# Transposed dense products as three passes of 256 columns into one sum, activation tiles at one place modulo 512 bytes

## The chip, the cores and the metric

The kernel runs on one core of one Trainium2 chip. The metric is the device time of one execution in microseconds (us), as the median of repeated runs.

## The reference

A two-layer trunk for 256 tokens of 2048 features, in float32:

```
for i in range(DEPTH):                      # DEPTH = 2
    h = rms_norm(x, mixer_norm[i])
    x = x + (diff_attention(h, ...) if i % 2 == 0 else gated_deltanet(h, ...))
    x = x + conv_ffn(rms_norm(x, ffn_norm[i]), ...)

def conv_ffn(h, w_up, conv_w, conv_b, w_down):
    u = causal_dwconv(h @ w_up, conv_w) + conv_b
    val, gate = jnp.split(u, 2, axis=-1)
    return (jax.nn.silu(gate) * val) @ w_down
```

Both mixers begin and end with dense products too: queries, keys, values and the output of the attention; queries, keys, values, gates, z and the output of the delta rule. Nearly all of the arithmetic is in these dense products with float32 weights.

## The kernel before, in words

Activations lie transposed, with the features on the 128 partitions and the 256 tokens along the free axis. A weight matrix comes in blocks of 256 output features and, within a block, in chunks of 512 KB (four tiles of 128 input features, `CK = 4`). `weights` (L67) issues the load of a chunk on SyncE's queue into `raw`, ScalarE casts it to the rounded part `whi` (L78), and VectorE subtracts to get the rest, `wlo` (L79). `raw` has four buffers, `whi` and `wlo` three each. An activation is split in the same way, and its two parts lie side by side in one tile of 512 columns: `h` (16 tiles h0 to h15, the input of a stage), `ac` (the attention's outputs, and the products of the gated MLP), `oc` (outputs of the delta rule). A product of two such numbers is the sum of three terms: hi times hi, lo (weight) times hi, hi times lo (activation).

`dense` (L92) forms a block. It has a PSUM bank of 512 columns for each of the two tiles of 128 features, numbered c, and for each tile k of the input and each c it does one *step*:

- in the form with two halves, two matmuls: `whi` against both parts at once, 512 columns wide (L112), and `wlo` against the first part, 256 columns wide, into the second half of the bank (L115). The two halves are added afterwards, in `merge` (L123) by ScalarE and VectorE, or in `add_out` (L232) by two additions.
- in the folded form (`fold=True`), three matmuls of 256 columns, all into the first half of the bank (L107, L108, L109), so that nothing is left to add.

Each matmul has its own load of 128 columns of weights into the array (PEld in the profile). The folded form is used in the gated delta rule, for the products with `w_in` (tiles `h`) and `w_out` (tiles `oc`), and for the very last block of the second MLP. All else that is transposed has two halves: `w_qk` (16 blocks of 32 steps), `w_o` (8 blocks of 32 steps), `w_up` of both MLPs (43 blocks of 32 steps each), `w_down` of both (8 blocks of 86 steps, the last block of the second MLP folded) and the gates of the delta rule (16 steps). That is 512 + 256 + 2752 + 1290 + 16 = 4826 steps with two halves and 1024 + 512 + 86 folded ones. `dense_tok` (L129), for values and z, is of another kind: there the weights move, 512 columns wide, and the activations are loaded into the array.

The stages follow each other: attention, MLP 0, delta rule, MLP 1. Matmuls between the dense ones (scores, norms, the small inverses of the delta rule) run as generators in the background, a step after each chunk (`tick`). In an MLP the only background work is `norm_stat` (L170): the sum over the partitions of the squares, with one matmul of 256 columns (L182) and two of one column (L184), after the third chunk of the stage. A scheduler orders the instructions of each engine.

Of the kernel before, what the change touches and what calls it, by code (L numbers as in the profile page):

```python
# [8 lines left out]
F32 = mybir.dt.float32  # L9
# [7 lines left out]
P = 128  # L17
# [8 lines left out]
class Trunk:  # L26
    """Activations lie transposed, features on the partitions and the 256 tokens along the free axis.

    A float32 operand of a dense product is split into two float32r parts (hi + lo, exact), and
    the passes carry hi * hi, hi * lo and lo * hi; the parts of an activation lie side by side, so  # L30
    that one pass of a weight's hi takes both, and the two halves of the sum are added after. Work that follows a dense block and needs the
    tensor engine again runs as a generator in the background, a step after each chunk of weights.
    """
# [33 lines left out]
    def weights(self, ap):  # L67
        """A chunk [128, k, n] of weights, in two parts."""
        nc = self.nc
        nk, n = ap.shape[1:]  # L70

        def tile_(tag, dt, bufs):
            t = self.wp.tile([P, CK * T], dt, tag=tag, name=tag, bufs=bufs)
            return t[:, :nk * n].rearrange("p (k n) -> p k n", n=n)

        raw, hi, lo = tile_("raw", F32, 4), tile_("whi", F32R, 3), tile_("wlo", F32R, 3)
        nc.sync.dma_start(raw, ap)
        nc.scalar.copy(hi, raw)  # L78
        nc.vector.tensor_tensor(lo, raw, hi.bitcast(F32), ALU.subtract)  # L79
# [10 lines left out]
    def dense(self, w, kt, acts, tiles=2, fold=False, lead=0):  # L90
        """out^T of 128 * tiles features, a PSUM bank for each 128, in two halves to be added,
        or (fold) in one, which spares the vector engine the sum."""  # L92
        nc = self.nc
        ps = self.banks()
        for k0, nk in self.chunks(kt, CK, lead):
            hi, lo = self.weights(w[:, k0:k0 + nk, :])
            steps = [(k, c) for k in range(nk) for c in range(tiles)]
            if fold and k0 + nk == kt:
                steps = [(k, c) for c in range(tiles) for k in range(nk)]
            for k, c in steps:  # L100
# [3 lines left out]

                def sole():
                    o = ps[:, c, :T]
                    nc.tensor.matmul(o, hi[:, k, s], a[:, 0, :], start=first, stop=False)  # L107
                    nc.tensor.matmul(o, lo[:, k, s], a[:, 0, :], start=False, stop=False)  # L108
                    nc.tensor.matmul(o, hi[:, k, s], a[:, 1, :], start=False, stop=last)  # L109

                def one():
                    nc.tensor.matmul(ps[:, c, :], hi[:, k, s], a, start=first, stop=last)  # L112

                def two():
                    nc.tensor.matmul(ps[:, c, T:], lo[:, k, s], a[:, 0, :], start=False, stop=False)  # L115

                for f in ((sole,) if fold else (one, two) if first else (two, one)):
                    f()
# [3 lines left out]
    def merge(self, ps, u):  # L122
        """The two halves of a dense block, added and divided by the rms of the tokens."""  # L123
        nc = self.nc
# [24 lines left out]
    def norm_tile(self, k, gcol):  # L149
        """One tile of x * gain, split; 1 / rms is applied after the products."""  # L150
# [19 lines left out]
    def norm_stat(self, wait=1):  # L170
        """1 / rms of each token, over all partitions and as columns."""
# [22 lines left out]
    def lnexp(self, inst):  # L194
        """After inst, the activations within run from the table set that has both functions."""
# [4 lines left out]
    def conv(self, out, u, taps, bias):  # L200
        """Causal depthwise convolution along the tokens."""
# [10 lines left out]
    def rsqrt(self, out, ps, n):  # L212
        """(ps / n + eps) ** -0.5"""
# [4 lines left out]
    def split(self, out, a):  # L218
        """Two float32r parts of a, out[:, 0] + out[:, 1] = a."""
# [3 lines left out]
    def total(self, out, parts):  # L223
        """Sums over the partitions of tiles, in two parts each, on every partition."""
# [6 lines left out]
    def add_out(self, blk, ps, done, fold=False):  # L231
        """x += a block of a projection, and what follows on each finished tile of x."""  # L232
        x = self.x[:, 2 * blk:2 * blk + 2, :]
        for i in range(1 if fold else 2):
            self.nc.vector.tensor_tensor(x, ps[:, :, i * T:(i + 1) * T], x, ALU.add)  # L235
# [5 lines left out]
    def project(self, w, kt, acts, done, final=False):  # L241
        """x += a projection; with final, the last block is left a tile at a time."""
# [3 lines left out]
        if final:  # L246
            ps = self.dense(w[n - 1], kt, acts, fold=True)
# [31 lines left out]
    def attention(self, w_qk, w_v, w_o, nh, dist_ap, ident_ap, qg, kg, lvec, sub, start, done, lambda_init):  # L279
        """qg, kg, lvec (4 columns), sub (2 columns): per-partition columns."""  # L280
        nc, mp = self.nc, self.mp
        with self.tc.tile_pool(name="at", bufs=1) as at:
# [5 lines left out]
            dist = at.tile([P, 384], F32, tag="dist", name="dist")  # L288
# [44 lines left out]
            def weigh(h, qn, kn, go, aT):  # L333
                """The differential attention weights of a head, keys on the partitions."""
# [77 lines left out]
    def gdn(self, w_gate, w_in, w_z, w_out, nb, hb, gate_ap, const_ap, hot_ap, conv_col, ng, done):  # L412
        """nb batches of hb query/key heads, each with two value heads; 128 wide, all of them.

        const_ap: identity, mask of the decays, upper triangle of ones.
        All 256 tokens are one chunk: u = (I + strict(K K^T . D) beta)^-1 v, o = (Q K^T . D) beta u, with
        D_ij = exp(G_i - G_j) for i >= j, beta within the exponent. Matrices lie transposed, as
        [second half of the keys: 128 queries | first half: 256 queries].
        """
# [5 lines left out]
        with tc.tile_pool(name="gd", bufs=1) as gd:  # L425
            self.spawn(self.norm_stat())
            con = gd.tile([P, 384], F32, tag="con", name="con")
# [18 lines left out]
            def lin(ps):  # L446
                u = gd.tile([P, 2, T], F32, tag="u", name="u", bufs=2)
                nc.vector.tensor_tensor(u, ps[:, :, :T], self.rstd.unsqueeze(1).to_broadcast([P, 2, T]), ALU.mult)
# [9 lines left out]
            def keys(hq, c, cc, b0, res):  # L458
                """Decayed K K^T and Q K^T of the two value heads of a query/key head."""
# [52 lines left out]
            def invert(cc, lqs, inv):  # L512
                """Inverses of the unit lower triangular 32x32 blocks on the diagonal, one in a partition."""
# [23 lines left out]
            def levels(TT, Ta, lts, ttc, tcc, m0):  # L537
                """Transposes of the inverses of the 128x128 blocks, from those of the 32x32 ones."""
# [54 lines left out]
            def group(gi, gr, lqs, inv, vt, ready, zts, acts):  # L593
                """Outputs of the value heads of a group, on their way to the last projection."""
# [67 lines left out]
            def out(b, acts):  # L662
                for blk in range(KD // 2):
                    ps = self.dense(w_out[b * (KD // 2) + blk], 2 * hb, lambda k: self.await_(acts, k), fold=True)
                    self.add_out(blk, ps, done if b == nb - 1 else None, True)
# [4 lines left out]
            for b in range(nb):  # L670
# [6 lines left out]
                for op, i in plan + [("v", i) for i in range(1, hb)]:  # L677
                    if op == "k":
                        hq = heads[i]
                        c = convs(lin(self.dense(w_in[hq * 2], KD, self.h_acts, fold=True)), (hq, nq + hq))  # L680
# [10 lines left out]
                    else:  # L691
# [7 lines left out]
                        c = convs(lin(self.dense(w_in[hq * 2 + 1], KD, self.h_acts, fold=True)),  # L699
# [7 lines left out]
    def gates(self, gd, pg, nv, gp, ident, triu, res):  # L707
        """Cumulated log decays as rows (two parts on 64 partitions), and negated, with the log of beta, as columns."""
# [200 lines left out]
```

## Time and profile before

| | |
|---|---|
| median of 3 runs | 2741.3 us (2741.16 to 2741.84) |
| profiled execution, first to last instruction (span) | 2741.9 us |
| TensorE (PE) busy | 2727.6 us, 99% |
| weight loads into the array (PEld) busy | 2433.3 us, 89% |
| VectorE (DVE) busy | 1920.3 us, 70% |
| ScalarE (ACT) busy | 1498.2 us, 55% |
| granted TensorE clock | 0.999 |
| read from HBM | 476.03 MB, 174 GB/s over the span |

The page gives no time of the profiled execution other than its span, which lies 0.6 us above the median of the runs. Rows of instruction groups read: line, engine, operation, output tile <- input tiles, shape, how many, busy time, mean duration in ns. Matmuls overlap: one that is recorded as 281 ns long can start 118 ns after the one before it. The duration of a record is therefore not what a matmul costs; the distance from start to start is.

### The profile page before, as it was taken

The numbers are of one execution on the slowest core, as the hardware profiler recorded it, in microseconds if no ns is written. First come the engines' busy times: TensorE is split into PE (matmuls) and PEld (weight loads), VectorE is DVE, ScalarE is ACT, GpSimd is POOL, SyncE is SP. The second block draws the span as 40 slices with busy tenths as digits, with TensorE's granted clock in tenths as the row PEclk, the third lists the DMA queues.
The fourth block names the chain that finished last, engine by engine and source line by source line (L and its number), as shares of the span: only waits on it lengthen the run. The fifth ranks groups of instructions, "written<-read, shape, count | busy, mean of one in ns | idle before, by whom it ended". The sixth has DMA issues, their size and how long they took to land.

```text
span 2741.9 us, 44249 instructions
## 1 busy us (share of the span) xinstructions
PE 2727.6 (99%) x17526; PEld 2433.3 (89%) x17526; DVE 1920.3 (70%) x2845; ACT 1498.2 (55%) x2094; POOL 117.0 (4%) x220
## 2 busy tenths in 40 slices
PE   8999999999999999999999999999999999999999
PEld 7888888888888888989989989989998888888888
DVE  7776577777777555679687687688677777776444
ACT  6665555555555444574564664574555555554333
POOL 0000000000000000022011011021000000000000
PEclk9999999999999999999999999999999999999999
DMA  6555565555555665655354454454455555556664
GB/s 210 170 166 173 156 193 186 185 186 188 187 185 188 187 187 185 187 158 180 116 164 168 131 170 146 154 167 157 152 185 187 186 186 186 188 187 194 191 195 151
DMA packets 135359, 481.00 MB, mean 175 GB/s; under 512 B 15344, under 2 KB 18416, under 8 KB 135152
## 3 DMA queue, kind: packets, MB, share of 16 engines
q1 hardware_dynamic: 134000, 475.57, 55.0%
q8 instruction: 137, 2.24, 0.3%
q10 hardware_dynamic: 1152, 2.61, 0.3%
q14 instruction: 70, 0.57, 0.1%
HBM read 476.03 MB, written 2.10 MB: 174 GB/s over the span
## 4 chain that ended last, share of the span: by engine, by line
PE 99%; DMA 0%; DVE 0%; ACT 0%; SPq 0%; issue 0%; DVEq 0%
PE ps L112 41%; PE ps L115 21%; PE ps L108 7%; PE ps L107 7%; PE ps L109 7%; PE ps L141 3%; PE ps L140 3%; PE ps L142 3%; PE mp L610 2%; PE mp L228 1%; PE mp L498 1%; PE mp L553 0%; PE mp L562 0%; PE mp L475 0%; PE mp L580 0%; PE mp L574 0%
## 5 line engine op out<-in xcount | busy, mean ns | idle before, releaser
L79 DVE TENSOR_TENSOR wlo<-raw,whi 128x1024 fp32r<-128x1024 f32 (+2 forms) x909 | 1107.1, 1218 | 571.5 <-ACT whi L78 568.7
L78 ACT CAST whi<-raw 128x1024 fp32r<-128x1024 f32 (+2 forms) x909 | 947.0, 1042 | 775.0 <-PE ps L112 475.5
L112 PE MATMUL ps<-h,whi 128*128 128x512 f32 x3280 | 1155.2, 398 | 6.1 <-DVE h L155 6.1
L115 PE MATMUL ps<-h,wlo 128*128 128x256 f32 x3280 | 908.4, 282 | 4.1 <-DVE wlo L79 4.1
L112 PEld LDWEIGHTS ps<-h,whi 128*128 128x128 f32 x3280 | 611.3, 188 | 147.7 <-DVE h L155 6.1
L115 PEld LDWEIGHTS ps<-h,wlo 128*128 128x128 f32 x3280 | 617.5, 188 | 14.1 <-DVE wlo L79 4.7
L112 PE MATMUL ps<-ac,whi 128*128 128x512 f32 x1546 | 543.5, 396 | 0.2 <-DVE x L235 0.2
L115 PE MATMUL ps<-ac,wlo 128*128 128x256 f32 x1546 | 430.2, 281 | 0.0
L112 PEld LDWEIGHTS ps<-ac,whi 128*128 128x128 f32 x1546 | 289.1, 188 | 68.7 <-ACT whi L78 0.5
L115 PEld LDWEIGHTS ps<-ac,wlo 128*128 128x128 f32 x1546 | 290.3, 188 | 2.0
L108 PE MATMUL ps<-h,wlo 128*128 128x256 f32 x1024 | 287.5, 281 | 0.0
L107 PE MATMUL ps<-h,whi 128*128 128x256 f32 x1024 | 286.1, 280 | 0.0
L109 PE MATMUL ps<-h,whi 128*128 128x256 f32 x1024 | 285.9, 279 | 0.0
L108 PEld LDWEIGHTS ps<-h,wlo 128*128 128x128 f32 x1024 | 193.7, 189 | 2.1
L107 PEld LDWEIGHTS ps<-h,whi 128*128 128x128 f32 x1024 | 193.1, 189 | 1.5 <-ACT whi L78 0.2
L109 PEld LDWEIGHTS ps<-h,whi 128*128 128x128 f32 x1024 | 193.2, 189 | 1.0
L140 PE MATMUL ps<-whi,h 128*128 128x512 f32 x384 | 151.5, 395 | 0.0
L141 PE MATMUL ps<-wlo,h 128*128 128x512 f32 x384 | 151.2, 394 | 0.0
L142 PE MATMUL ps<-whi,h 128*128 128x512 f32 x384 | 150.8, 393 | 0.0
L108 PE MATMUL ps<-oc,wlo 128*128 128x256 f32 x512 | 144.2, 282 | 0.0
L107 PE MATMUL ps<-oc,whi 128*128 128x256 f32 x512 | 144.1, 282 | 0.0
L109 PE MATMUL ps<-oc,whi 128*128 128x256 f32 x512 | 143.9, 281 | 0.0
(215 smaller groups left out, 2710.6 us busy)
## 6 DMA issues: line engine op xcount, KB each, us to landing
raw<-w_up SPq DMA_DIRECT2D x344, 512.0 KB, 4.4
raw<-w_down SPq DMA_DIRECT2D x160, 512.0 KB, 3.5
raw<-w_in SPq DMA_DIRECT2D x128, 512.0 KB, 4.4
raw<-w_z SPq DMA_DIRECT2D x64, 512.0 KB, 3.7
raw<-w_out SPq DMA_DIRECT2D x64, 512.0 KB, 3.8
raw<-w_qk SPq DMA_DIRECT2D x63, 512.0 KB, 3.9
raw<-w_v SPq DMA_DIRECT2D x32, 512.0 KB, 3.5
raw<-w_o SPq DMA_DIRECT2D x32, 512.0 KB, 4.7
```

The costliest lines, as they stand in the source:

```text
L78: nc.scalar.copy(hi, raw)
L79: nc.vector.tensor_tensor(lo, raw, hi.bitcast(F32), ALU.subtract)
L107: nc.tensor.matmul(o, hi[:, k, s], a[:, 0, :], start=first, stop=False)
L108: nc.tensor.matmul(o, lo[:, k, s], a[:, 0, :], start=False, stop=False)
L109: nc.tensor.matmul(o, hi[:, k, s], a[:, 1, :], start=False, stop=last)
L112: nc.tensor.matmul(ps[:, c, :], hi[:, k, s], a, start=first, stop=last)
L115: nc.tensor.matmul(ps[:, c, T:], lo[:, k, s], a[:, 0, :], start=False, stop=False)
L140: nc.tensor.matmul(ps[:, c, :], ah, hi[:, k, :], start=first, stop=False)
L141: nc.tensor.matmul(ps[:, c, :], ah, lo[:, k, :], start=False, stop=False)
L142: nc.tensor.matmul(ps[:, c, :], al, hi[:, k, :], start=False, stop=last)
L228: last = self.nc.tensor.matmul(out, self.onesr, p[:, j], start=i + j == 0, stop=i + j == n)
L610: nc.tensor.matmul(p[:, v, :], l(v), r[:, v, :], start=i == 0, stop=i == len(terms) - 1)
```

## The change

`dense` loses the form with two halves and its switch `fold`: every step is now three matmuls of 256 columns into one half of a bank, and in the last chunk of every block all steps of the first tile c come ahead of those of the second, which before only folded blocks did. `merge` becomes one multiplication on VectorE, `add_out` one addition, and the gates' sum goes. Three tiles that are allocated ahead of others in their pools are made longer, `fcols` by 64 columns, `dist` by 72 and `con` by 64, of which nothing is used. Those behind them move by so much: in the attention `ac` from byte 384 to byte 160 modulo 512 within a partition, in the MLPs `ac` from 416 to 160, in the delta rule `oc` from 416 to 160. The tiles `h` were and are at 160, the weights `whi` and `wlo` at 480.

```
-    def dense(self, w, kt, acts, tiles=2, fold=False, lead=0):
+    def dense(self, w, kt, acts, tiles=2, lead=0):
...
             steps = [(k, c) for k in range(nk) for c in range(tiles)]
-            if fold and k0 + nk == kt:
+            if k0 + nk == kt:
                 steps = [(k, c) for c in range(tiles) for k in range(nk)]
...
-                def sole():
-                    o = ps[:, c, :T]
-                    nc.tensor.matmul(o, hi[:, k, s], a[:, 0, :], start=first, stop=False)
-                    nc.tensor.matmul(o, lo[:, k, s], a[:, 0, :], start=False, stop=False)
-                    nc.tensor.matmul(o, hi[:, k, s], a[:, 1, :], start=False, stop=last)
-
-                def one():
-                    nc.tensor.matmul(ps[:, c, :], hi[:, k, s], a, start=first, stop=last)
-
-                def two():
-                    nc.tensor.matmul(ps[:, c, T:], lo[:, k, s], a[:, 0, :], start=False, stop=False)
-
-                for f in ((sole,) if fold else (one, two) if first else (two, one)):
-                    f()
+                o = ps[:, c, :T]
+                nc.tensor.matmul(o, hi[:, k, s], a[:, 0, :], start=first, stop=False)
+                nc.tensor.matmul(o, lo[:, k, s], a[:, 0, :], start=False, stop=False)
+                nc.tensor.matmul(o, hi[:, k, s], a[:, 1, :], start=False, stop=last)
...
     def merge(self, ps, u):
-        nc.scalar.copy(u, ps[:, :, T:])
-        nc.vector.tensor_tensor(u, ps[:, :, :T], u, ALU.add)
-        nc.vector.tensor_tensor(u, u, self.rstd.unsqueeze(1).to_broadcast([P, 2, T]), ALU.mult)
+        self.nc.vector.tensor_tensor(u, ps[:, :, :T], self.rstd.unsqueeze(1).to_broadcast([P, 2, T]), ALU.mult)
...
-        for i in range(1 if fold else 2):
-            self.nc.vector.tensor_tensor(x, ps[:, :, i * T:(i + 1) * T], x, ALU.add)
+        self.nc.vector.tensor_tensor(x, ps[:, :, :T], x, ALU.add)
...
-            cols = fp.tile([P, 4, 2, nj], F32, tag="fcols", name="fcols")
+            cols = fp.tile([P, 8 * nj + 64], F32, tag="fcols", name="fcols")[:, :8 * nj]
+            cols = cols.rearrange("p (t h j) -> p t h j", t=4, h=2)
...
-            dist = at.tile([P, 384], F32, tag="dist", name="dist")
+            dist = at.tile([P, 384 + 72], F32, tag="dist", name="dist")[:, :384]
...
-            con = gd.tile([P, 384], F32, tag="con", name="con")
+            con = gd.tile([P, 384 + 64], F32, tag="con", name="con")[:, :384]
```

The first place is on TensorE near the end of the first block of MLP 0, where `norm_stat` comes in. The names h_86 to h_90 are the tiles h11 to h15. Before:

```order
L115 MATMUL ps<-h_88,wlo 128x256
L112 MATMUL ps<-h_88,whi 128x512
L182 MATMUL mp<-ss,ones 128x256
L184 MATMUL mp<-ones,ss 128x1 x2
L115 MATMUL ps<-h_89,wlo 128x256
L112 MATMUL ps<-h_89,whi 128x512
```

and in the changed program, at the same place:

```order
L106 MATMUL ps<-h_86,whi 128x256
L104 MATMUL ps<-h_87,whi 128x256
L167 MATMUL mp<-ss,ones 128x256
L169 MATMUL mp<-ones,ss 128x1 x2
L105 MATMUL ps<-h_87,wlo 128x256
L106 MATMUL ps<-h_87,whi 128x256
L104 MATMUL ps<-h_88,whi 128x256
```

The three matmuls of `norm_stat` have moved a little forward and stand now between passes of 256 columns; from here to the end of MLP 0 no other background matmul follows in either program.

The second place is on TensorE where `norm_stat` comes in at MLP 1. Before:

```order
L115 MATMUL ps<-h_82,wlo 128x256
L112 MATMUL ps<-h_82,whi 128x512
L182 MATMUL mp<-ss,ones 128x256
L184 MATMUL mp<-ones,ss 128x1 x2
L115 MATMUL ps<-h_83,wlo 128x256
```

and in the changed program:

```order
L106 MATMUL ps<-h_82,whi 128x256
L167 MATMUL mp<-ss,ones 128x256
L169 MATMUL mp<-ones,ss 128x1
L104 MATMUL ps<-h_83,whi 128x256
L169 MATMUL mp<-ones,ss 128x1
L105 MATMUL ps<-h_83,wlo 128x256
```

Here a dense pass now stands between the two matmuls of one column. What follows is again free of background work to the end of the kernel.

More of the change, by code (lines that the diff above doesn't have):

```diff
@@ L246, in project @@
         if final:
-            ps = self.dense(w[n - 1], kt, acts, fold=True)
+            ps = self.dense(w[n - 1], kt, acts)
             for c in range(2):
@@ L447, in lin @@
                 u = gd.tile([P, 2, T], F32, tag="u", name="u", bufs=2)
-                nc.vector.tensor_tensor(u, ps[:, :, :T], self.rstd.unsqueeze(1).to_broadcast([P, 2, T]), ALU.mult)
+                self.merge(ps, u)
                 return u
@@ L663, in out @@
                 for blk in range(KD // 2):
-                    ps = self.dense(w_out[b * (KD // 2) + blk], 2 * hb, lambda k: self.await_(acts, k), fold=True)
-                    self.add_out(blk, ps, done if b == nb - 1 else None, True)
+                    ps = self.dense(w_out[b * (KD // 2) + blk], 2 * hb, lambda k: self.await_(acts, k))
+                    self.add_out(blk, ps, done if b == nb - 1 else None)
             pg = self.dense(w_gate, KD, self.h_acts, tiles=1)
@@ L679, in gdn @@
                         hq = heads[i]
-                        c = convs(lin(self.dense(w_in[hq * 2], KD, self.h_acts, fold=True)), (hq, nq + hq))
+                        c = convs(lin(self.dense(w_in[hq * 2], KD, self.h_acts)), (hq, nq + hq))
                         self.spawn(keys(hq, c, cc, 2 * i, lqs))
@@ L698, in gdn @@
                         hq = heads[i]
-                        c = convs(lin(self.dense(w_in[hq * 2 + 1], KD, self.h_acts, fold=True)),
+                        c = convs(lin(self.dense(w_in[hq * 2 + 1], KD, self.h_acts)),
                                   (2 * nq + 2 * hq, 2 * nq + 2 * hq + 1))
```

7 lines of the change are left out of this document (2 added, 5 removed).

## The prediction

> **What bounds the kernel now.** I read the page from the top: busy times first, then the chain that ended last, then what TensorE (PE) waited for.
>
> ```profile
> PE 2727.6 (99%) x17526; PEld 2433.3 (89%) x17526; DVE 1920.3 (70%) x2845; ACT 1498.2 (55%) x2094; POOL 117.0 (4%) x220
> ...
> PE 99%; DMA 0%; DVE 0%; ACT 0%; SPq 0%; issue 0%; DVEq 0%
> ```
>
> TensorE is busy for 99% of the span and the chain runs through it alone. Its list of waits holds three entries:
>
> ```profile
> PE ps L112 <- DVE h L155: 6.1, 1, 6.1
> PE ps L115 <- DVE wlo L79: 4.1, 1, 4.1
> PE ps L112 <- DVE x L235: 0.2, 1, 0.2
> ```
>
> That is 10.4 us in all, and nothing can be won there. ScalarE waits for TensorE:
>
> ```profile
> L78 ACT CAST whi<-raw 128x1024 fp32r<-128x1024 f32 (+2 forms) x909 | 947.0, 1042 | 775.0 <-PE ps L112 475.5
> L79 DVE TENSOR_TENSOR wlo<-raw,whi 128x1024 fp32r<-128x1024 f32 (+2 forms) x909 | 1107.1, 1218 | 571.5 <-ACT whi L78 568.7
> ```
>
> So the time is the number of dense steps times the distance between them. Everything hangs on how far apart three 256-column passes stand, against one of 512 and one of 256.
>
> **The change, part by part.** The old pair first: the list by line of code, cut to stretches without background work. It gives the count and the first and last start; the rows are MLP 0's `w_up` and `w_down`, MLP 1's `w_up` and `w_down`, and the attention's `w_o`.
>
> ```profile
> L112 PE MATMUL ps<-h,whi x1101: 388/397/398, 505.8 to 894.0; 128*128 128x512 f32 x184
> L112 PE MATMUL ps<-ac,whi x288: 388/397/398, 894.3 to 995.7; 128*128 128x512 f32 x144
> L112 PE MATMUL ps<-h,whi x1304: 388/397/398, 2029.9 to 2489.8; 128*128 128x512 f32 x187
> L112 PE MATMUL ps<-ac,whi x585: 388/397/398, 2499.6 to 2705.9; 128*128 128x512 f32 x195
> L112 PE MATMUL ps<-ac,whi x148: 391/392/395, 348.9 to 399.9; 128*128 128x512 f32 x148
> ```
>
> One step is 388.2 us / 1100 = 352.9 ns, 101.4 / 287 = 353.3, 459.9 / 1303 = 353.0 and 206.3 / 584 = 353.3; in `w_o`, whose tiles lie elsewhere, 51.0 / 147 = 346.9.
>
> Now the three passes, where the kernel uses them already: two stretches of the delta rule on `h`, one on `oc`, and the last block of MLP 1.
>
> ```profile
> L108 PE MATMUL ps<-h,wlo x101: 276/276/277, 1257.9 to 1291.9; 128*128 128x256 f32 x101
> L108 PE MATMUL ps<-h,wlo x95: 276/276/277, 1429.9 to 1461.9; 128*128 128x256 f32 x95
> L107 PE MATMUL ps<-oc,whi x114: 281/281/281, 1963.9 to 2003.9; 128*128 128x256 f32 x114
> L109 PE MATMUL ps<-ac,whi x86: 280/281/281, 2707.8 to 2737.8; 128*128 128x256 f32 x86
> ```
>
> The first two give 34.0 / 100 = 340.0 and 32.0 / 94 = 340.4 ns a step; the others 40.0 / 113 = 354.0 and 30.0 / 85 = 352.9, together 70.0 / 198 = 353.5. **The three passes have two cadences**, 340 and 353.5 ns, and hold one of them through a whole stretch. The recorded length tells them apart: 276 ns in the fast one, 281 in the slow one. The slow one is as good as the old pair, the fast one saves 13 ns a step. The prediction is a matter of which cadence the long stretches get.
>
> What the fast cadence would save, stage by stage:
>
> - `w_up`, 86 blocks x 32 = 2752 steps x (352.9 - 340.0) = 35.5 us;
> - `w_down`, 15 blocks x 86 = 1290 steps x 13.3 = 17.2 us, and the last block, which is folded but slow today, 86 x 12.9 = 1.1 us;
> - so each MLP is worth 26.9 us (0: 1376 x 12.9 + 688 x 13.3; 1: 1376 x 12.9 + 602 x 13.3 + 1.1);
> - `w_qk`, 512 steps that background matmuls interrupt: 6.6 us all fast, -0.3 all slow; I take half, 3.3;
> - `w_o`, 256 steps: from 346.9 to 340 is 1.8 us won, to 353.5 1.7 lost; I take 0;
> - the delta rule's 1536 steps have three passes already, but each interruption may fall out anew. All 13.5 ns apart, 1536 steps span 20.7 us; I take 0, with 5 us either way as the range.
>
> Which cadence comes up is settled in the first few passes behind an interruption. Two entries from the timeline of TensorE, the first behind `norm_stat` in the delta rule, the second behind an interruption of the folded passes:
>
> ```profile
> 1143.32 0.50 PE L184 MATMUL mp<-ones,ss 128*128 128x1 f32 x4
> 1143.68 0.36 PE L107 MATMUL ps<-h,whi 128*128 128x256 f32 x1
> 1143.88 0.28 PE L108 MATMUL ps<-h,wlo 128*128 128x256 f32 x1
> 1144.00 0.28 PE L109 MATMUL ps<-h,whi 128*128 128x256 f32 x1
> 1144.12 0.28 PE L107 MATMUL ps<-h,whi 128*128 128x256 f32 x1
> ...
> 1144.71 0.28 PE L109 MATMUL ps<-h,whi 128*128 128x256 f32 x1
> ```
>
> ```profile
> 1324.10 0.37 PE L108 MATMUL ps<-h,wlo 128*128 128x256 f32 x1
> 1324.30 0.28 PE L109 MATMUL ps<-h,whi 128*128 128x256 f32 x1
> 1324.42 0.28 PE L107 MATMUL ps<-h,whi 128*128 128x256 f32 x1
> ...
> 1325.55 0.28 PE L108 MATMUL ps<-h,wlo 128*128 128x256 f32 x1
> ```
>
> The first settles at (1144.71 - 1144.00) / 6 = 118 ns a pass, the second, after the same 0.20 us and 0.12 us, at (1325.55 - 1324.42) / 10 = 113 ns. On the same tiles `h`, the same weights' places and the same distances the outcome differs, so the place modulo 512 bytes doesn't settle it alone. Nor does it forbid either: `oc` and `ac` at 416 are shown slow above, `h` at 160 fast and slow. The means over the whole delta rule say how common the two are:
>
> ```profile
> L107 PE MATMUL ps<-h,whi 128*128 128x256 f32 x1024 | 286.1, 280 | 0.0
> L109 PE MATMUL ps<-h,whi 128*128 128x256 f32 x1024 | 285.9, 279 | 0.0
> L107 PE MATMUL ps<-oc,whi 128*128 128x256 f32 x512 | 144.1, 282 | 0.0
> ```
>
> Between 276 and 281, a mean of 279 stands for at least (281 - 279) / 5 = 40% fast on `h`, and more, since passes next to an interruption are recorded as 360 ns and longer and pull it up; on `oc` 282 says that the slow one prevails. The change puts every activation at `h`'s place, 160, so I go by `h`: an estimate of six in ten for the fast cadence. Within an MLP no interruption follows `norm_stat` (the order of the changed program shows none, and none of TensorE's three waits lies in one), so that one entry decides some 27 us. The entry behind `norm_stat` shown above came out slow, once; that holds me at no more than six in ten.
>
> The rest is hidden. Work taken from VectorE (two operations of some 690 ns a block) and ScalarE (one of 586) lay under the matmuls; at 340 ns a step a chunk of eight steps lasts 2.72 us, against 1.04 us of ScalarE and 1.22 of VectorE for it. Loads must rise from 512 KB in 2.82 us, 186 GB/s, to 193 GB/s; the window of the second fast stretch moves 195 already:
>
> ```profile
> 1430.00:1479.00 49.00, 49.00 (x435) 49.00 (x434) 46.22 (x85) 24.49 (x30) 2.11 (x4) 1.00 0.58 195
> ```
>
> There, too, TensorE is busy throughout, with VectorE at 46 of 49 us: neither feed nor VectorE is late next. The 4826 added matmuls and weight loads cost what the cadence says: at the slow one 353.5 - 352.9 = 0.6 ns a step (2.9 us over 4826), at the fast one the gain above.
>
> The Trainium skill ("TensorE: Matmul & The Clock Gate", Back-to-back issue gap) speaks against the change: it gives N / 2.4 + 2.5 ns for a matmul of N columns, so 325.0 ns for the old step and 327.6 for the new one, and the sum by it would be 4826 x 2.5 = 12 us slower. The trace doesn't bear out the level (352.9 for the old step) nor, in the fast stretches, the sign (340.0).
>
> **Sum, for both MLPs fast:** 35.5 + 17.2 + 1.1 + 3.3 = 57.1 us off the span of 2741.9, and off the median of the runs, 0.6 lower, 2741.3 - 57.1 = **2684.2 us**.
>
> **The rivals.**
>
> - *One MLP falls into the slow cadence*: 2741.3 - 26.9 - 3.3 = 2711. For it: entries differ on equal tiles, and `norm_stat` enters the two MLPs in different orders. Against: the two differ in one pass only.
> - *Both do*, so that the change does nothing but replace one cadence of 353 by another: 3.3 gained in `w_qk`, 2752 x 0.6 + 1290 x 0.2 = 1.9 lost, 2740, with the delta rule's 5 us either way. For it: the slow entry shown above, and the last block, slow for all of 30 us.
> - *Slower: the slow cadence everywhere.* The place is the first passes behind each interruption, the price 13.5 ns for each step that is fast today. If the moved order of background work and the shifted `oc` turned the fast half of the delta rule's 1536 steps (768 x 13.5 = 10.4 us), and `w_o` went from 346.9 to 353.5 (1.7), with 1.9 in the MLPs and 0.3 in `w_qk`: 2741.3 + 14.3 = 2756. It decides against me from the point where more than a third of the delta rule turns while both MLPs are slow. Against it: the entries behind `w_z` blocks were fast in both stretches shown.
> - *A cost for every matmul start*, which the short folded stretches don't show and the long ones would. The nearest rows bound it by 5 ns, the difference between a slow pass's record and a fast one's; taking half of that once for each added pass, 4826 x 2.5 = 12 us, it gives 2753. The skill's rule above gives the same. Against it: the last block ran 258 passes at 353 ns a step, not more.
>
> **How the numbers follow.** Both MLPs fast 0.42, one 0.25, neither 0.20, slow everywhere 0.08, a cost for every start 0.05. The likeliest is 2684, by itself 2676 to 2692 with the attention's and the delta rule's spread. The range must take in the cases of one and of none: 2676 to 2746, which leaves out the two slower cases, 0.13. A difference of 0.2%, 5.5 us, is about what a measurement of this kernel can tell from no change. Faster by more: 0.42 + 0.25 + a fifth of "neither" = 0.71; within: 0.15; slower: 0.14.
>
> **What would show it.** In the changed profile the records of the MLPs' passes are 276 ns long and first and last starts give 340 ns a step if the fast cadence holds; 281 and 353.5 if not. A whole MLP should show one length from `norm_stat` to its end; a switch in mid-stretch, or 276 in `w_up` and 281 in `w_down`, would break the step that one entry decides a stage. TensorE's waits should stay near 10 us; a wait for `wlo` in the MLPs would mean that the feed had become late. A step over 354 ns would speak for a cost of each start.

## The result and the profile after

| | before | after |
|---|---|---|
| median of 12 runs each, taken side by side | 2742.01 us (2740.93 to 2743.80) | 2744.27 us (2742.55 to 2746.16) |
| ratio after / before | | 1.0007, 95% interval 0.9999 to 1.0016 |
| profiled execution, span | 2741.9 us | 2742.3 us |
| granted TensorE clock | 0.999 | 0.999 |

The change makes no difference that can be measured; the forecast was a gain of 57 us. First the busy times on the page of the changed kernel:

```profile
PE 2728.7 (100%) x22352; PEld 2656.1 (97%) x22352; DVE 1857.5 (68%) x2719; ACT 1457.5 (53%) x1994; POOL 118.4 (4%) x220
```

The 4826 added matmuls are there (22352 against 17526), TensorE bounds the kernel as before, and VectorE and ScalarE have lost work (1857.5 us against 1920.3, 1457.5 against 1498.2) that nobody waited for. The longest of TensorE's waits (us in all, times, longest):

```profile
PE ps L104 <- ACT h L139: 5.3, 1, 5.3
```

With it, five waits make 9.7 us, against 10.4 before: the feed is not late. So the answer lies in the cadence. The list by line of the changed kernel, cut to stretches without background work (minimum, median and maximum length in ns, first and last start in us). The rows are the end of `w_o`, MLP 0's `w_up` and `w_down`, the end of the last `w_out`, MLP 1's `w_up` and `w_down`:

```profile
L104 PE MATMUL ps<-ac,whi x213: 281/281/281, 324.8 to 399.7; 128*128 128x256 f32 x107
L104 PE MATMUL ps<-h,whi x1336: 281/281/281, 415.1 to 886.8; 128*128 128x256 f32 x191
L106 PE MATMUL ps<-ac,whi x651: 281/281/281, 900.1 to 1129.7; 128*128 128x256 f32 x163
L104 PE MATMUL ps<-oc,whi x97: 281/281/281, 1970.0 to 2004.0; 128*128 128x256 f32 x97
L104 PE MATMUL ps<-h,whi x1303: 281/281/281, 2029.9 to 2490.0; 128*128 128x256 f32 x187
L104 PE MATMUL ps<-ac,whi x644: 281/281/281, 2509.7 to 2736.9; 128*128 128x256 f32 x161
```

Not one record of 276 ns. Both MLPs run at 471.7 / 1335 = 353.3, 229.6 / 650 = 353.2, 460.1 / 1302 = 353.4 and 227.2 / 643 = 353.3 ns a step: the slow cadence, from `norm_stat` to the end. But the two stretches *ahead* of the MLPs are slow as well, 74.9 / 212 = 353.3 in `w_o` and 34.0 / 96 = 354 in `w_out`. That was the first hint at what follows.

To see what each stage gained, I read where it begins: the first start on `h` and the last on `ac`, in windows around the borders. Before:

```profile
L112 PE MATMUL ps<-h,whi x89: 388/397/399, 407.8 to 439.8; 128*128 128x512 f32 x89
...
L112 PE MATMUL ps<-ac,whi x106: 388/397/398, 1099.9 to 1137.0; 128*128 128x512 f32 x106
...
L112 PE MATMUL ps<-h,whi x87: 388/397/398, 2008.5 to 2039.8; 128*128 128x512 f32 x87
```

and after:

```profile
L104 PE MATMUL ps<-h,whi x97: 281/281/281, 405.0 to 439.8; 128*128 128x256 f32 x97
...
L106 PE MATMUL ps<-ac,whi x100: 281/281/281, 1100.1 to 1135.0; 128*128 128x256 f32 x100
...
L104 PE MATMUL ps<-h,whi x88: 281/281/364, 2008.2 to 2039.8; 128*128 128x256 f32 x88
```

| stage (us) | before | after | difference | forecast |
|---|---|---|---|---|
| attention | 407.8 | 405.0 | -2.8 | -3.3 |
| MLP 0 | 729.2 | 730.0 | +0.8 | -26.9 |
| delta rule | 871.5 | 873.2 | +1.7 | 0 +- 5 |
| MLP 1, to the end of the span | 733.4 | 734.1 | +0.7 | -26.9 |

Of the 57.5 us of span that are missing, 55.3 are missing in the two MLPs.

### The profile page after: what moved, and what is told of

Same layout as the page of the kernel before. It is cut to its first block, busy times and chain, and to the rows that moved or that the text cites. A ratio compares the mean times of both kernels' runs of the same rounds, so it can differ in the third digit from the quotient of the medians.

```text
span 2742.3 us, 53669 instructions
## 1 busy us (share of the span) xinstructions
PE 2728.7 (100%) x22352; PEld 2656.1 (97%) x22352; DVE 1857.5 (68%) x2719; ACT 1457.5 (53%) x1994; POOL 118.4 (4%) x220
## 4 chain that ended last, share of the span: by engine, by line
PE 99%; ACT 0%; DVE 0%; DMA 0%; issue 0%; SPq 0%; DVEq 0%; ACTq 0%
PE ps L105 28%; PE ps L104 27%; PE ps L106 27%; PE ps L125 3%; PE ps L127 3%; PE ps L126 3%; PE mp L595 2%; PE mp L213 1%; PE mp L483 1%; PE mp L538 0%; PE mp L547 0%; PE mp L460 0%; PE mp L559 0%; PE mp L565 0%; PE mp L574 0%; PE mp L482 0%
## 5 line engine op out<-in xcount | busy, mean ns | idle before, releaser
L104 PE MATMUL ps<-h,whi 128*128 128x256 f32 x4304 | 1208.2, 281 | 9.0 <-ACT h L139 5.3
L105 PE MATMUL ps<-h,wlo 128*128 128x256 f32 x4304 | 1209.1, 281 | 0.5 <-DVE wlo L79 0.4
L106 PE MATMUL ps<-h,whi 128*128 128x256 f32 x4304 | 1207.8, 281 | 0.0
L104 PEld LDWEIGHTS ps<-h,whi 128*128 128x128 f32 x4304 | 820.7, 191 | 11.6 <-ACT h L139 5.3
L106 PEld LDWEIGHTS ps<-h,whi 128*128 128x128 f32 x4304 | 809.9, 188 | 1.4
L104 PE MATMUL ps<-ac,whi 128*128 128x256 f32 x1632 | 458.4, 281 | 0.0
L105 PE MATMUL ps<-ac,wlo 128*128 128x256 f32 x1632 | 458.3, 281 | 0.0
L106 PE MATMUL ps<-ac,whi 128*128 128x256 f32 x1632 | 458.2, 281 | 0.0
L104 PEld LDWEIGHTS ps<-ac,whi 128*128 128x128 f32 x1632 | 312.2, 191 | 0.0
L105 PEld LDWEIGHTS ps<-ac,wlo 128*128 128x128 f32 x1632 | 307.2, 188 | 0.0
L106 PEld LDWEIGHTS ps<-ac,whi 128*128 128x128 f32 x1632 | 306.2, 188 | 0.0
L194 DVE SCALAR_TENSOR_TENSOR cv<-u,fcols,cv 128x255 f32<-128x255 f32 (+1 forms) x344 | 142.8, 478 | 0.0
L112 DVE TENSOR_TENSOR u<-ps,rstd 128x512 f32<-128x512 f32 x118 | 81.4, 690 | 51.0 <-PE ps L106 50.9
```

The lines of the kernel that those rows point to most:

```text
L112: self.nc.vector.tensor_tensor(u, ps[:, :, :T], self.rstd.unsqueeze(1).to_broadcast([P, 2, T]), ALU.mult)
L194: nc.vector.scalar_tensor_tensor(out[:, j:], u[:, :T - j], taps[n - 1 - j], out[:, j:], ALU.mult, ALU.add)
```

## The experiments

The theory formed on this result: **the cadence is carried**. `norm_stat` doesn't choose one, it hands on what it finds, and what it found had been set in `w_o` and `w_out`. The rivals: the entry behind `norm_stat` decides, as the prediction had it; the place of the tiles decides; a long stretch can't hold the fast cadence, because it wears out or is not fed.

### The places, with and without the three passes

The first three kernels and the tenth separate the two parts of the change. `e1_passes_only` is the changed kernel without the longer tiles; `e10_places_only` is the kernel before with them.

```diff
-            cols = fp.tile([P, 8 * nj + 64], F32, tag="fcols", name="fcols")[:, :8 * nj]
+            cols = fp.tile([P, 8 * nj + 0], F32, tag="fcols", name="fcols")[:, :8 * nj]
...
-            dist = at.tile([P, 384 + 72], F32, tag="dist", name="dist")[:, :384]
+            dist = at.tile([P, 384 + 0], F32, tag="dist", name="dist")[:, :384]
...
-            con = gd.tile([P, 384 + 64], F32, tag="con", name="con")[:, :384]
+            con = gd.tile([P, 384 + 0], F32, tag="con", name="con")[:, :384]
```

> Three passes everywhere, but no tile is made longer: h stays at 160 modulo 512 bytes, ac lies at 384 in the attention and at 416 in the MLPs, oc at 416. Theory 'entry' (the first passes behind an interruption choose between 340 and 353.5 ns a step, the place doesn't matter): the entries behind norm_stat are those of the changed kernel, so both MLPs are at 353.5 ns a step throughout and the time is 2744 us, within 4 us for the attention and the delta rule. Theory 'place' (the place modulo 512 bytes sets the cadence): w_up as in the changed kernel, since h has not moved, but w_down and w_o differ from it: 346.9 or 340 ns a step in w_o, and something other than 353.5 in w_down.

Measured: 2741.53 us, ratio to before 0.9998 (0.9988 to 1.0007). MLP 0's `w_down`, with `ac` at 416 here, by line:

```profile
L104 PE MATMUL ps<-ac,whi x652: 281/281/281, 899.9 to 1129.9; 128*128 128x256 f32 x163
```

230.0 / 651 = 353.3, as with `ac` at 160. `w_o`, with `ac` at 384 here, ran at 355.7 ns a step (211 records, first starts from 325.0 to 399.7 us), neither 340 nor 346.9. The passes alone bring nothing either, and in the MLPs the move from 416 to 160 did nothing.

> The other part of the change alone: the kernel before, with two halves, and the three tiles made longer, so that ac and oc lie at 160 modulo 512 bytes. By the runs so far 160 and 416 are alike, and only the attention's ac comes from a place of another kind (384): w_o from 346.9 to 353 ns a step, 256 x 6.1 = 1.6 us more, 2744 us; the MLPs at 352.9 as before. If 160 did help the two halves, they would fall below 352.9.

Measured: 2742.69 us, ratio 1.0003 (0.9993 to 1.0013). The longer tiles alone bring nothing. One group did answer, `w_o`, which they move from 384 to 160:

```profile
L112 PE MATMUL ps<-ac,whi x145: 388/397/398, 348.8 to 399.7; 128*128 128x512 f32 x145
```

50.9 / 144 = 353.5 ns a step, where the prediction's row at 384 gave 346.9.

`e2_passes_384` is the changed kernel with `h`, `ac` and `oc` all at 384, `e3_halves_384` the kernel before with the same places:

```diff
-        self.eps = self.cp.tile([P, 1], F32, tag="eps", name="eps")
+        self.eps = self.cp.tile([P, 1 + 56], F32, tag="eps", name="eps")[:, :1]
...
-        self.onesr = self.cp.tile([P, P], F32R, tag="onesr", name="onesr")
+        self.onesr = self.cp.tile([P, P + 72], F32R, tag="onesr", name="onesr")[:, :P]
...
+            cols = fp.tile([P, 8 * nj + 120], F32, tag="fcols", name="fcols")[:, :8 * nj]
...
+            con = gd.tile([P, 384 + 120], F32, tag="con", name="con")[:, :384]
```

> Three passes everywhere, h, ac and oc all at 384 modulo 512 bytes instead of 160, the weights where they were. Theory 'entry': the same two cadences, 340 and 353.5 ns a step, and a time near 2744 us unless the entry behind norm_stat falls out the other way (27 us less for each MLP for which it does). Theory 'place': the cadences themselves change, as w_o at 384 had 346.9 ns with two halves against 352.9 elsewhere; if nothing but the better one is left, 340 ns in the MLPs and some 2690 us.

Measured: 2767.59 us, ratio 1.0088 (1.0071 to 1.0105): slower by 0.9%. Both MLPs' `w_up`, by line:

```profile
L104 PE MATMUL ps<-h,whi x1348: 277/280/282, 415.0 to 890.0; 128*128 128x256 f32 x193
...
L104 PE MATMUL ps<-h,whi x1349: 277/281/283, 2034.9 to 2514.8; 128*128 128x256 f32 x193
```

475.0 / 1347 = 352.6, which takes in the 0.8 us of `norm_stat` (352.0 without it), and 479.9 / 1348 = 356.0. The three passes have other cadences at this place: every stretch of more than 30 passes free of waits ran at about 117.3, 118.7 or 120.0 ns a pass, none at 113.3, which is 340 a step. Against the changed kernel the span is 24.6 us longer, and 16.3 of them lie in the delta rule, whose fast stretches are gone; MLP 0 is 2.7 shorter, MLP 1 5.6 longer.

> The kernel before with two halves, h, ac and oc at 384 modulo 512 bytes. Theory 'place': every step with two halves takes 346.9 ns, as w_o does in the kernel before: 2752 x 6.0 + 1290 x 6.4 + 512 x 6.0 = 28 us less, 2714 us. Theory 'entry', by which 346.9 in w_o is a matter of how that stage was entered: 352.9 ns in the MLPs and 2742 us.

Measured: 2733.34 us, ratio 0.9967 (0.9954 to 0.9980): faster than both kernels. The borders of its delta rule, and `w_up` of MLP 1 by itself:

```profile
L112 PE MATMUL ps<-ac,whi x95: 391/392/395, 1089.9 to 1122.5; 128*128 128x512 f32 x95
...
L112 PE MATMUL ps<-h,whi x141: 389/392/398, 2010.3 to 2059.8; 128*128 128x512 f32 x141
...
L112 PE MATMUL ps<-h,whi x1299: 391/392/395, 2029.7 to 2479.9; 128*128 128x512 f32 x186
```

450.2 / 1298 = 346.8 ns a step. MLP 1 takes 721.2 us of the span of 2731.5, 12.2 less than before. But the delta rule, whose passes were folded already, takes 2010.3 - 1122.5 = 887.8, 16.3 more, and eats what more than one MLP wins; the expectation of 2714 us had left it out. So the place sets *which* cadences there are, in opposite directions for the two forms; at 160 and at 416, it doesn't set which of the two comes up.

### Which products switch the cadence

`e4_survey` throws one product of eight kinds into the changed kernel's queue ahead of each block of `w_up` from the third on, the kind by the block's number modulo 9 (0: none). Its results go to a PSUM tile that nothing reads. Cut to three kinds:

```diff
+    def kick(self, kind):
...
+        elif kind == 2:
+            nc.tensor.matmul(p, self.onesr, h, start=True, stop=True)
+        elif kind == 3:
+            nc.tensor.matmul(p[:, :P], self.ones, x[:, 0, :P], start=True, stop=True)
...
+        elif kind == 7:
+            nc.tensor.matmul(p[:32, :32], x[:32, 0, :32], self.ones[:32, :32], start=True, stop=True)
...
             for j in range(nj):
+                if j % 9 and j > 1:
+                    self.kick(j % 9)
```

> The changed kernel with a short product thrown in ahead of most blocks of w_up in both MLPs, in turn one of eight kinds (from 32x32 to three of 512 columns), whose result nothing reads. Some 36 of them in each MLP at 0.2 to 0.7 us add about 20 us. Theory 'entry': blocks behind some kinds run at 340 ns a step and behind others at 353.5, the same kind alike each time and in both MLPs; each block at 340 wins 0.43 us back. Theory 'place': all blocks stay at 353.5, since no tile moves, and the time is 20 us up.

Measured: 2751.37 us in a single run. The timeline of TensorE in MLP 0 (start in us, length, line), around the first product of 512 columns and the first float32 product of 128:

```profile
427.63 0.28 PE L105 MATMUL ps<-h,wlo 128*128 128x256 f32 x1
...
428.10 0.28 PE L106 MATMUL ps<-h,whi 128*128 128x256 f32 x1
428.22 0.39 PE L162 MATMUL mp<-h,onesr 128*128 128x512 f32 x1
428.45 0.28 PE L104 MATMUL ps<-h,whi 128*128 128x256 f32 x1
...
429.59 0.28 PE L105 MATMUL ps<-h,wlo 128*128 128x256 f32 x1
...
439.34 0.38 PE L164 MATMUL mp<-x,ones 128*128 128x128 f32 x2
439.68 0.28 PE L105 MATMUL ps<-h,wlo 128*128 128x256 f32 x1
...
440.74 0.28 PE L105 MATMUL ps<-h,wlo 128*128 128x256 f32 x1
```

Ahead of the product of 512, four passes in 0.47 us, 118 each; behind it, ten in 1.14 us, 114. Behind the product of 128, nine in 1.06 us, 118. A kind that stood by itself did the same each time, in both MLPs, and every block kept what it got, over 96 or 192 passes:

| thrown in | cadence of the block behind it |
|---|---|
| one product of 512 columns, float32r | fast, 9 of 9 (the first met the slow one) |
| three of 512, float32r | fast, 10 of 10 |
| one of 32x32, float32 | fast, 8 of 8, each from the slow one |
| one of 128 columns, float32 | slow, 9 of 9, each from the fast one |
| two of 1 column, float32 | slow, 9 of 9 (all met the slow one) |
| one of 256 columns, float32r, `onesr` as weights | slow, 10 of 10, from the fast one |
| one of 64x64; one of 256 columns with 64 rows of weights | met only the fast one and left it, 8 each |
| none | as the block before |

(In MLP 1 the scheduler put the first three, one each of 512, 128 and 1 column, next to each other; the slow cadence came out, and they are not counted.) So an interruption can set the cadence, in `w_up` predictably by its kind, and some kinds leave it. Kind alone is not the whole rule. In the delta rule of the changed kernel a single L213 of 512 columns with `onesr`, a kind of the table, stands six times ahead of 16 or more passes, each time 4 to 13 passes behind another background product: four of these stretches are fast, and two are slow (83 passes from 1556.9 us on, 92 from 1771.8 us on, 118 ns each). What else decides stays open. The table does fit what had been found ahead of MLP 0. In the changed kernel the attention's last background products are eight of L213, of 256 columns with `onesr` as weights, in groups of one, three, one and three with two to six passes between them. The timeline around them, with the last group:

```profile
319.83 0.28 PE L105 MATMUL ps<-ac,wlo 128*128 128x256 f32 x1
...
321.98 0.28 PE L106 MATMUL ps<-ac,whi 128*128 128x256 f32 x1
...
323.86 0.51 PE L213 MATMUL mp<-sqp,onesr 128*128 128x256 f32 x3
324.20 0.28 PE L105 MATMUL ps<-ac,wlo 128*128 128x256 f32 x1
...
325.96 0.28 PE L105 MATMUL ps<-ac,wlo 128*128 128x256 f32 x1
```

Ahead, 19 passes in 2.15 us, 113.2 each; behind, 15 in 1.76 us, 117.3. `w_o` had been fast and went slow here, as the survey's kind with `onesr` does; which of the eight turned it can't be read from so few passes between them. The rest of `w_o` and all of MLP 0 followed at that cadence.

### A product of 32x32 inside the MLPs

`e5_kick_mlp` is the changed kernel with one such product ahead of the second block of `w_up` in each MLP:

```diff
+    def kick(self):
+        nc = self.nc
+        nc.tensor.matmul(self.mp()[:32, :32], self.x[:32, 0, :32], self.ones[:32, :32], start=True, stop=True)
...
             for j in range(nj):
+                if j == 1:
+                    self.kick()
```

> The changed kernel with one 32x32 product thrown in behind norm_stat in each MLP, ahead of the second block of w_up; nothing reads its result. In the survey this kind was followed by 340 ns a step each time. Theory 'entry': both MLPs run at 340 ns from there to their ends, 2 x (42 x 32 + 688) steps x 13.3 = 54 us less than the changed kernel's 2744, for 0.5 us of added products: 2691 us. Rival 'fast stretches wear out' (the longest seen has some 450 passes, an MLP has over 6000): the cadence falls back to 353.5 on the way, and the time lies between 2691 and 2744, with the switch to be seen in mid-stretch.

Measured: 2717.31 us, ratio 0.9910 (0.9893 to 0.9926). `w_up` of MLP 0, its `w_down`, and `w_up` of MLP 1, by line:

```profile
L104 PE MATMUL ps<-h,whi x1334: 276/276/276, 420.9 to 874.2; 128*128 128x256 f32 x191
L104 PE MATMUL ps<-ac,whi x678: 276/276/276, 874.5 to 1104.7; 128*128 128x256 f32 x170
...
L104 PE MATMUL ps<-h,whi x1324: 281/281/281, 2000.1 to 2467.5; 128*128 128x256 f32 x190
```

MLP 0 is fast to its end, 453.3 / 1333 = 340.1 and 230.2 / 677 = 340.0: a long stretch holds the fast cadence and is fed at it. That rival is out. MLP 1 stayed slow, 467.4 / 1323 = 353.3, and this part of the expectation failed. The timeline shows where the scheduler put the product there:

```profile
1986.98 0.28 PE L173 MATMUL mp<-ones,ss 128*128 128x1 f32 x2
1987.18 0.24 PE L157 MATMUL mp<-ones,x 32*32 32x32 f32 x2
1987.36 0.38 PE L105 MATMUL ps<-h,wlo 128*128 128x256 f32 x1
```

It stands right between `norm_stat`'s last product (L173) and the next pass, with no pass between the two. Where it stood 23 passes behind `norm_stat`, in MLP 0, it switched. Why it doesn't in this order I can't say.

`e6_places` is `e5_kick_mlp` with every fourth `ac` tile of the MLPs 32 bytes longer, so that each chunk of `w_down` has its own place, 160, 192, ... 480:

```diff
-                ac = fp.tile([P, 2, T], F32R, tag=f"ac{j}", name="ac")
+                ac = fp.tile([P, 2 * T + (8 if j % 4 == 3 else 0)], F32R, tag=f"ac{j}", name="ac")[:, :2 * T]
+                ac = ac.rearrange("p (i t) -> p i t", i=2)
```

> As the run with one product behind norm_stat in each MLP, but the tiles ac of the MLPs lie at eleven places, each group of four 32 bytes further on than the last, from 160 to 480 modulo 512 bytes, so that every chunk of w_down has its own. w_up at 340 ns a step. Theory 'place and entry' (the place sets which cadences there are, the entry chooses among them): the chunks of w_down differ by place, alike in all blocks of both MLPs, those at 160, 288 and 416 able to keep 340 ns and those at 256 and 384 at 350 to 357, as the run with all tiles at 384 had. Theory 'entry alone': w_down stays at 340 ns over all eleven places.

Measured: 2727.51 us in a single run, some 10 more than `e5_kick_mlp`. In its timeline, the first pass of the chunks at 160, 192 and 224 in one block:

```profile
905.16 0.29 PE L104 MATMUL ps<-ac,whi 128*128 128x256 f32 x1
...
907.90 0.28 PE L104 MATMUL ps<-ac,whi 128*128 128x256 f32 x1
...
910.74 0.28 PE L104 MATMUL ps<-ac,whi 128*128 128x256 f32 x1
```

A chunk has 24 passes: 2.74 / 24 = 114 ns at 160, 2.84 / 24 = 118 at 192; read in the same way, 113.7 at 416 and 117.4 to 119.8 at each of the others, 288 among them, and each chunk gave the same within 0.8 ns in all 16 blocks of both MLPs but for one, MLP 1's first at 160 (117.8), which came out of the slow cadence: the product in MLP 1 had not switched `w_up` here either. Of the places tried, with the weights at 480, only 160 and 416, 256 bytes apart, have the fast one; and it comes back by itself after chunks that don't. In MLP 1 it even came up anew: the chunk at 416 of the first block was fast, though all before it had been slow. So passing through tiles at other places can switch the cadence too, with no other product in between.

`e7_halves_kick` is the kernel before with the same product as in `e5_kick_mlp`.

> The kernel before, with two halves, and the same 32x32 product behind norm_stat in both MLPs. If the old pair has a fast cadence as well that it was never started into, the MLPs fall below 352.9 ns a step, by up to 13, and the time by up to 54 us. If only three equal passes have one, which I expect, w_up keeps 352.9 ns a step and the time 2742 to 2743 us.

Measured: 2741.63 us in a single run. `w_up` of MLP 0:

```profile
L112 PE MATMUL ps<-h,whi x1304: 388/397/398, 424.9 to 884.7; 128*128 128x512 f32 x187
```

459.8 / 1303 = 352.9, as before: the product did nothing to the form with two halves here. What it wins needs the three passes.

### The product ahead of the MLPs

`e8_kick_more` has products ahead of the second and third block of `w_o` and of the fourth block of the last `w_out`, besides those in the MLPs. `e9_kick_ahead` has *only* these three, and none in the MLPs:

```diff
         for b in range(n - final):
+            if b in kicks:
+                self.kick()
...
-            self.project(w_o, 2 * nh, lambda k: self.await_(outs, k), done)
+            self.project(w_o, 2 * nh, lambda k: self.await_(outs, k), done, kicks=(1, 2))
...
+                    if b == nb - 1 and blk == 3:
+                        self.kick()
```

> As the run with one product behind norm_stat in each MLP, and three more of them: ahead of the second and third block of w_o and of the fourth block of the last w_out. Theory 'entry': the slow ends of w_o (some 180 steps) and of the last w_out (some 140 steps) go to 340 ns as well, 320 x 13.3 = 4 us less than the run with one product in each MLP, for 0.8 us: about 2688 us. Rival: the order of the attention's background work moves and eats it; 2691 or more.

Measured: 2687.67 us, ratio 0.9800 (0.9786 to 0.9815). `w_up` of MLP 1, slow in `e5_kick_mlp` in spite of its product, runs at 340.0 ns a step (1309 records of 276 ns in 444.7 us): the same order of `norm_stat` and product, but out of a fast `w_out`.

> The changed kernel with 32x32 products only ahead of the MLPs: before the second and third block of w_o and before the fourth block of the last w_out; none in the MLPs themselves. Theory 'carried' (norm_stat keeps the cadence that it finds; the changed kernel's MLPs are slow because w_o and the last w_out end slowly): both MLPs at 340 ns a step from their first block to their last, some 2687 us. Rival 'norm_stat resets' (its matmuls of one column are followed by the slow cadence whatever was before, as the prediction had it): w_o's end and the last w_out at 340, both MLPs at 353.5, some 2740 us.

Measured: 2686.22 us, ratio 0.9796 (0.9781 to 0.9811), some 2% faster than the kernels before and after; `e8_kick_more` is within the noise of it. The borders of its stages:

```profile
L104 PE MATMUL ps<-h,whi x110: 275/277/281, 401.9 to 439.9; 128*128 128x256 f32 x110
...
L106 PE MATMUL ps<-ac,whi x14: 276/276/277, 1100.0 to 1104.5; 128*128 128x256 f32 x14
...
L104 PE MATMUL ps<-h,whi x181: 275/277/367, 1977.7 to 2039.8; 128*128 128x256 f32 x181
```

Against before (span 2684.4 against 2741.9): attention 401.9, 5.9 less; MLP 0 702.6, 26.6 less; delta rule 873.2, 1.7 more; MLP 1 706.7, 26.7 less. Its `norm_stat` in MLP 0, in the timeline:

```profile
408.70 0.28 PE L104 MATMUL ps<-h,whi 128*128 128x256 f32 x1
...
410.06 0.28 PE L104 MATMUL ps<-h,whi 128*128 128x256 f32 x1
410.17 0.59 PE L171 MATMUL mp<-ss,ones 128*128 128x256 f32 x2
410.61 0.50 PE L173 MATMUL mp<-ones,ss 128*128 128x1 f32 x4
...
411.29 0.28 PE L104 MATMUL ps<-h,whi 128*128 128x256 f32 x1
...
412.00 0.28 PE L104 MATMUL ps<-h,whi 128*128 128x256 f32 x1
...
412.79 0.28 PE L105 MATMUL ps<-h,wlo 128*128 128x256 f32 x1
```

Ahead of it 12 passes in 1.36 us, 113 each. Behind it six in 0.71 us, 118 each, and then seven in 0.79 us, 113 again. In the changed kernel, the same three matmuls enter between the same kinds of pass, and the cadence is slow ahead of and behind them:

```profile
412.18 0.28 PE L105 MATMUL ps<-h,wlo 128*128 128x256 f32 x1
...
413.47 0.28 PE L104 MATMUL ps<-h,whi 128*128 128x256 f32 x1
413.59 0.59 PE L167 MATMUL mp<-ss,ones 128*128 128x256 f32 x2
...
414.70 0.28 PE L104 MATMUL ps<-h,whi 128*128 128x256 f32 x1
...
415.88 0.28 PE L105 MATMUL ps<-h,wlo 128*128 128x256 f32 x1
```

11 passes in 1.29 us, 117 each, and ten in 1.18 us, 118. One entry, two outcomes, each the one that held before it. That is the theory, shown: nothing was changed in either MLP, TensorE's order in them is the same matmul by matmul in both traces, and both turned. The other traces agree. In the changed kernel, `e1_passes_only`, `e5_kick_mlp`, `e8_kick_more`, `e9_kick_ahead` and `e11_kick_no_places` `norm_stat` enters MLP 0, the delta rule and MLP 1, 18 entries in all, 9 out of the slow cadence and 9 out of the fast one, and each time the cadence behind it is the one ahead. (In MLP 1 of `e5_kick_mlp`, `e8_kick_more` and `e11_kick_no_places` the thrown-in product follows directly.)

`e11_kick_no_places` is `e8_kick_more` without the longer tiles, which are taken away as in `e1_passes_only`.

> Three passes with the five added products, but no tile made longer: ac at 384 in w_o and at 416 in the MLPs, oc at 416. If 160 and 416 are alike, both MLPs hold 340 ns a step once they have it, w_down at 416 too, and only w_o stays at 350 ns or more for want of its place: 256 x 13 to 18 = 3 to 5 us above the 2688 of the run with the longer tiles, 2691 to 2693. If one place for all were needed, w_down would fall to 353.5 and cost 2 x 9 us more: 2710.

Measured: 2687.19 us, ratio 0.9802 (0.9787 to 0.9816), as `e8_kick_more` with them, and not the 3 to 5 us above it that were expected. `w_o` did lose, 94.5 us against 91.8 from its first start to its last, but it began 2.7 us earlier (308.9 against 311.6 us), which the expectation did not have; why is open. The second half of the change isn't needed for the gain.

## Why the prediction was wrong, point by point

**Right: that TensorE's distance from start to start is all that counts**, that neither feed nor VectorE would be late, and that the three passes have two cadences, 340 and 353.5, told apart by records of 276 and 281 ns. The worth of the fast one was right too: 26.9 us were put down for each MLP, and `e9_kick_ahead` wins 26.6 and 26.7. The sum for both MLPs fast, 57.1 us, is met by it with 57.5 of span, in part by luck: its attention won 5.9 where 3.3 were put down, its delta rule lost 1.7 where nothing was, and three products are added that the change doesn't have.

**Wrong: "that one entry decides some 27 us".** This is the step that failed. It took `norm_stat` for the place where the cadence is drawn, on "an estimate of six in ten". But the entry hands on what it finds. The outcome was settled ahead of it, in `w_o` behind L213 and in the last `w_out`, where the forecast put no more than 1.8 us and a part of the delta rule's 5 at stake. In time, what came was the rival "replace one cadence of 353 by another", priced at 2740; but that rival, too, left the cadence to the entry.

Two readings led there. The estimate by mean record lengths took the delta rule's passes as draws of one lot, while each stood behind an interruption of its own kind. Its share was not far off: of the starts on `h` there, 2000 of 2931 follow at some 113 ns. But a share says nothing about a single entry that doesn't draw. And the two entries compared in the prediction differed in more than the outcome: the one behind `norm_stat` came out of a stretch in the form with two halves, the other out of passes of 256. What stood *ahead* of the interruption wasn't read. Six passes behind it are also too short a look: in `e9_kick_ahead` they are at 118 ns in a stretch that is fast.

**Right as far as it went: that "the place modulo 512 bytes doesn't settle it alone".** 160 and 416 show both cadences. But other places have no fast one at all (`e2_passes_384`, `e6_places`), which the prediction didn't say.

**Right: no cost for every start.** The step went from 352.9 to 353.3 ns, 0.4 x 4826 = 1.9 us, not the 12 us of that rival, which would be a ratio of 1.0044 and lies outside the interval. The rule of the Trainium skill ("TensorE: Matmul & The Clock Gate", Back-to-back issue gap), some 2.5 ns beside N / 2.4 for each matmul, gives those 12 us as an estimate (325.0 and 327.5 ns a step). The section states it for a matmul by itself and says that in a stream of weight loads and matmuls both set the spacing. The runs, which are such streams, don't bear the rule out, neither by the level (113.3 or 117.8 ns for 256 columns, where it has 109) nor by the sum.

**The small terms.** The attention won 2.8 us where 3.3 were put down; in it `w_o` went from 346.9 to 353.3, the loss that the range allowed for. The delta rule lost 1.7, within its 5.

**What stays open.** Why in `w_up` a product of 512 columns or of 32x32 makes the following passes fast and one of 128 or of 256 with `onesr` makes them slow, why the first of these doesn't always do so in the delta rule, and what holds the state, the profile doesn't show. Nor is the last step ahead of MLP 1 traced as closely as L213: `w_out` was slow behind its last background products, and the product thrown in behind them turned it, with MLP 1.

## What to carry to other kernels

Read cadence from start to start, over dozens of passes, and look at what it was *ahead of* an interruption as well as behind: where a stretch may run at two speeds, the one it has may have been set a stage earlier. Before putting a chance on such an outcome, sort the interruptions in the trace by their kind. And where an edit should have won and didn't, a tiny product in the right place (three of 32x32 here) can tell, at almost no cost, whether the faster state is there to be had.

## What the hardware showed that was not expected

- Equal passes of 256 columns run at 113.3 or 117.8 ns, and keep it over more than 6000 passes, through three matmuls of another kind, and from stage to stage.
- A single product of 32x32 in float32, recorded as 0.24 us in all, made the 6000 passes behind it in MLP 0 faster by 4%.
- The place of the moving tile within a partition changes the cadence, with the weights at 480: 114 ns at 160 and 416, 117.4 to 119.8 at the nine others tried. At 384 the form with two halves gains (346.8 a step against 352.9) where the three passes lose (352.0 to 356.0 in the MLPs against 340).
